# The last down-projection stage of the first FFN as seven products of sums of quarters, in a decoder trunk on one core

## The chip, the cores and the metric

The kernel runs on one core of one Trainium2 chip. The metric is device time in microseconds (us), the median of several executions. The core's engines work side by side, each through its own queue in order: TensorE (PE) multiplies matrices into PSUM, VectorE (DVE) and ScalarE (ACT) work on elements, GpSimd (POOL) and SyncE (SP) mostly issue transfers (DMA).

## What is computed

A decoder trunk of 512 tokens and width 1024: retention, gated ConvFFN, stick-breaking attention, gated ConvFFN, a final norm. All in float32. Only the FFN and its surroundings matter here:

```python
def _conv_ffn(h, w_up, conv_w, conv_b, w_down):
    u = h @ w_up
    u = lax.conv_general_dilated(u, conv_w[:, None, :].astype(u.dtype), window_strides=(1,),
                                 padding=[(CONV_W - 1, 0)],
    ...
    gate, val = jnp.split(u, 2, axis=-1)
    return (jax.nn.silu(gate) * val) @ w_down
    ...
        x = x + _conv_ffn(_rmsnorm(x, ffn_norm[i]), ffn_w_up[i], ffn_conv_w[i],
                          ffn_conv_b[i], ffn_w_down[i])
```

`D_FF` is 2816, so an FFN has 22 feature tiles of 128 (each a gate and a value of the up-projection), and the down-projection multiplies 22 x 128 features into 8 row tiles of x.

## The kernel before

**Precision.** Every float32 operand is split into `hi` (rounded to the matmul's type, a cast on ScalarE) and `lo` (the remainder, a subtraction on VectorE); a product is three matmuls, hi x hi, hi x lo, lo x hi.

**Layout.** x stands transposed: 8 tiles of 128 features x 512 tokens (`head` is tile 0, then x1 to x7; the rows below call all of them x). Weights come from HBM in chunks. `chunk` (L159 on) loads one into a `raw` slot on SyncE's queue, casts it to `hi` and subtracts for `lo`. Each of the three has a ring of five slots: four in a pool that lives as long as the kernel and a fifth, whose names carry a plus (`hi+`, `lo+`), in the pool of the present phase (`ret`, `ffn`, `sb`). When a phase ends, the next one's tiles take over its memory, and the fifth slot with them.

**An FFN** (`ffn`). `first4` multiplies the first two feature tiles' weights, eight k steps (one x tile each), into four banks. The other up-projections follow, 24 matmuls of 512 columns each. `ffn_act` evicts a bank, applies the three taps and the gate, and prepares the feature as an operand of the down-projection. The down-projection is done in three stages, features 0 to 7, 8 to 15 and 16 to 21 in the first FFN, and its result is added to x stage by stage. The first two are fast stages: `fast_down` computes, for each half of the rows of x (four tiles), seven products of sums of quarters in place of eight products of quarters, a Strassen scheme. A product has 256 token columns (`quarter`, L666), and the banks are added to or subtracted from x on VectorE (L676), 14 instructions of 256 columns per half. For that a pair of features needs 7 x 256 columns of operand: four quarters, and three further sums that VectorE forms (L645 to L647), then a cast (L649) and a subtraction (L650) of 1792 columns (`oh`, `ol`). The corresponding sums of weight quarters are formed ahead of time in HBM: `weight_sums` has POOL issue transfers, half of them accumulating, in the order of the table `ORDER`. The fast stages run two features after their last one.

The third stage is ordinary: a feature's operand is a cast and a subtraction of 512 columns (L637, L638), and `down` takes, for each of the 8 row tiles, one weight chunk of 128x768 and 18 matmuls of 512 columns, adds the bank to x (`add_to_x`, L228), and at once prepares the next norm from that tile: `norm_split` (L155 on ScalarE, L156 on VectorE: the tile times its gain, as hi and lo) and `norm_sum` (a square on ScalarE, L254, added up on VectorE, L255).

**What follows it.** `first4("sfirst")` of the stick-breaking layer takes one chunk and one split x tile in each k step. The norm's factor (one over a root of the mean square, one per token) is applied only to the results: `rsqrt` sums the squares over partitions with two matmuls on TensorE (L262), takes the root on ScalarE and the reciprocal on VectorE. It stands before the matmuls of one of the k steps.

**Order.** A scheduler arranges each engine's instructions when the program is built; on the chip each queue runs in the order so set.

Of the kernel before, what the change touches and what calls it, by code (L numbers as in the profile page):

```python
# [18 lines left out]
KD = D // P  # L19
# [6 lines left out]
NF = DFF // P  # L26
CH = 1024
STAGES = (((0, 8), (8, 16), (16, 22)), ((0, 8), (8, 14), (14, 18)))
FAST = (2, 2)
TAIL = 18  # L30
Q = S // 2
HALF = S // 2
# [1 line left out]

ORDER = (
    (("fqk", 0, 1), ("fv", 0, 2), ("fg", 0, 1), ("fqk", 1, 1), ("fg", 1, 1), ("fast0_0", 0, 2), ("fast0_1", 0, 2)),
    (("fast1_0", 0, 2), ("fast1_1", 0, 2)),
)
WARM = 3
RAW = 4  # L40
# [4 lines left out]
class Kernel:  # L45
# [133 lines left out]
    def first4(self, name, load=False):  # L179


        ps = [self.att() for _ in range(4)]
        for k in range(KD):
            w = self.wchunk(name, k, S)
            if load:
                if k:
                    self.nc.sync.dma_start(self.x[k], self.t["xT"][k])
                self.norm_split(k, 0, load)
                self.norm_sum(k)
            if k == (KD - 1 if load else KD // 2):  # L190
                self.r = self.rsqrt(self.sq, D, "rr")
            for i, (a, b) in enumerate(((0, 0), (1, 0), (0, 1))):
                for m in range(4):
                    self.nc.tensor.matmul(  # L194
                        ps[m], w[a][:, m * P : (m + 1) * P], self.xs[k][b], start=k + i == 0, stop=k == KD - 1 and i == 2
                    )
        return ps
# [426 lines left out]
    def ffn_act(self, l, f, ps):  # L624
# [7 lines left out]
        nc.vector.tensor_mul(y, g, v)  # L632
        if f >= STAGES[l][FAST[l] - 1][1]:
            if f % 2 == 0:
# [46 lines left out]
    def ffn(self, l, last):  # L681
        a, s = [], 0
        first = self.first4(f"ufirst{l}")
        if l == 0:
            self.weight_sums(ORDER[1], self.r)
        self.phase("ffn")
        for f in range(NF):
            a.append(self.ffn_act(l, f, first[2 * f : 2 * f + 2] if f < 2 else (None, None)))
            if f == 1:
                self.swap_pool()  # L690
            if s < 2 and f == STAGES[l][s][1] + 1:
                lo, hi = STAGES[l][s]
                for half in range(2):
                    self.fast_down(l, s, a[lo + 1 : hi : 2], half)
                s += 1
        self.swap_pool()
        self.down(l, a, s, last)
        if last is not None:
            self.phase("sb")
        return a  # L700
# [248 lines left out]
def _quarters(w, nk):  # L949

    n = w.shape[1] // (4 * P)
    w = w.reshape(nk, 2, P, n, 2, 2, P)
    return w.transpose(3, 5, 1, 2, 4, 0, 6).reshape(n, 4, P, 2 * nk * P)
# [15 lines left out]
def _layout(x, ret_norm, ret_w_in, ret_w_out, sb_norm, sb_w_in, sb_w_out,  # L969
# [26 lines left out]
    for l in range(2):  # L996
# [4 lines left out]
        for s, (lo, hi) in enumerate(STAGES[l]):  # L1001
            w = ffn_w_down[l][lo * P : hi * P]
            if s < FAST[l]:
                a[f"fast{l}_{s}"] = _quarters(w, (hi - lo) // 2)
# [29 lines left out]
```

## Time and profile before

| | before |
|---|---|
| median of 3 runs | 1352.93 us (1352.07 to 1353.94) |
| the profiled execution, time | 1353.2 us |
| the profiled execution, span | 1351.4 us |
| TensorE busy | 1337.1 us, 99% of the span |
| VectorE busy | 1012.0 us, 75% |
| ScalarE busy | 664.2 us, 49% |
| matmuls | 7086 |

Busy time of TensorE says that a matmul was under way; matmuls overlap (one of 512 columns shows 0.39 us), so their rate is read from the distance of their starts in the timeline. An engine's idle time counts only where TensorE waits for it in turn. Times in the rows are us from the span's start.

### The profile page before, as it was taken

The page shows a single profiled execution, that of the slowest core. Times are in us where ns is not written, and L with a number is a line of the kernel's source. Part 1 is how long each engine was busy: PE and PEld are TensorE (multiplying, and loading weights), DVE is VectorE, ACT ScalarE, POOL GpSimd, SP SyncE. Part 2 cuts the span into 40 slices and gives each one's busy share as a digit, 9 for nine tenths or more (in the row PEclk, how much of TensorE's full clock was granted, in tenths as well). Part 3 has the DMA queues.
Part 4 walks back from the last instruction along what each step waited for, and adds up shares of the span by engine and source line. Part 5 has one row for each costly group of instructions (what it writes and reads, how often), then busy time and mean ns, then how long its engine had stood idle before and what let it go on. Part 6 is the DMA issues. An engine that isn't in the chain of part 4 may idle for free.

```text
span 1351.4 us, 18540 instructions
## 1 busy us (share of the span) xinstructions
PE 1337.1 (99%) x7086; PEld 1142.2 (85%) x7086; DVE 1012.0 (75%) x1401; ACT 664.2 (49%) x987; POOL 111.4 (8%) x191
## 2 busy tenths in 40 slices
PE   9999999999999999999999999999999999999997
PEld 7888889899988889888988887777888899898887
DVE  7777677688769887678676628888699886787665
ACT  5444535574655444444344437666375443444434
POOL 1222221000002210000000011221000000000000
PEclk9999999999999999999999999999999999999999
DMA  9999999834338976334521654544143345235121
GB/s 319 302 292 279 278 305 293 257 106 154 102 123 269 284 203 188 109 94 123 166 72 47 186 142 146 148 117 111 40 141 109 97 140 157 84 111 173 53 70 63
DMA packets 67962, 217.96 MB, mean 161 GB/s; under 512 B 7969, under 2 KB 10145, under 8 KB 67873
## 3 DMA queue, kind: packets, MB, share of 16 engines
q1 hardware_dynamic: 45616, 145.97, 34.1%
q0 software_dynamic: 20736, 69.22, 20.7%
q10 hardware_dynamic: 1520, 1.58, 0.3%
q8 instruction: 56, 0.92, 0.3%
q14 instruction: 34, 0.27, 0.1%
HBM read 202.06 MB, written 58.72 MB: 193 GB/s over the span
## 4 chain that ended last, share of the span: by engine, by line
PE 96%; DVE 2%; ACT 1%; issue 0%; DMA 0%; DVEq 0%
PE acc L171 20%; PE acc L172 20%; PE acc L173 20%; PE att L194 7%; PE x L666 6%; PE att L666 5%; PE z L666 3%; PE acc L666 2%; PE att L374 2%; PE att L172 2%; PE att L171 2%; PE att L173 2%; PE one L789 1%; PE tp L781 1%; PE z L761 1%; DVE sg L766 1%
## 5 line engine op out<-in xcount | busy, mean ns | idle before, releaser
L164 ACT CAST hi<-raw 128x1024 fp32r<-128x1024 f32 (+2 forms) x255 | 248.1, 974 | 341.2 <-PE acc L172 184.2
L165 DVE TENSOR_TENSOR lo<-raw,hi 128x1024 fp32r<-128x1024 f32 (+2 forms) x255 | 285.4, 1123 | 74.6 <-ACT hi L164 73.0
L172 PE MATMUL acc<-xl,hi 128*128 128x512 f32 x696 | 271.3, 390 | 0.0
L171 PE MATMUL acc<-xh,hi 128*128 128x512 f32 x696 | 271.2, 390 | 0.0
L173 PE MATMUL acc<-xh,lo 128*128 128x512 f32 x696 | 271.1, 390 | 0.0
L173 PEld LDWEIGHTS acc<-xh,lo 128*128 128x128 f32 x696 | 130.7, 188 | 27.3
L171 PEld LDWEIGHTS acc<-xh,hi 128*128 128x128 f32 x696 | 130.7, 188 | 26.2
L172 PEld LDWEIGHTS acc<-xl,hi 128*128 128x128 f32 x696 | 130.7, 188 | 26.1 <-issue 0.2
L621 DVE SCALAR_TENSOR_TENSOR tt<-tt,vec,tt 128x511 f32<-128x511 f32 (+1 forms) x176 | 130.8, 748 | 3.9 <-ACT tt L619 1.4
L618 DVE TENSOR_TENSOR tt<-acc,rr 128x512 f32<-128x512 f32 x80 | 55.1, 689 | 73.0 <-PE acc L173 73.0
L619 ACT ACTIVATE tt<-tt,vec 128x512 f32<-128x512 f32 x88 | 71.5, 815 | 9.5 <-DVE tt L618 8.4
L666 PE MATMUL att<-xo,hi 128*128 128x256 f32 x384 | 70.1, 284 | 0.0
L228 DVE TENSOR_TENSOR x<-x,acc 128x512 f32<-128x512 f32 x63 | 42.9, 687 | 33.8 <-PE acc L173 33.8
L766 DVE TENSOR_TENSOR_SCAN sg<-sg,diag 128x512 f32<-128x512 f32 (+3 forms) x64 | 52.5, 821 | 13.2 <-ACT sg L763 13.2
L666 PEld LDWEIGHTS att<-xo,hi 128*128 128x128 f32 x384 | 59.8, 190 | 0.2
L628 ACT ACTIVATE tt<-tt 128x512 f32<-128x512 f32 x44 | 27.8, 631 | 55.2 <-DVE tt L621 55.2
L666 PE MATMUL att<-xo,lo 128*128 128x256 f32 x192 | 54.3, 283 | 0.0
L666 PE MATMUL x<-oh,hi 128*128 128x256 f32 x188 | 53.5, 285 | 0.0
L666 PE MATMUL x<-oh,lo 128*128 128x256 f32 x188 | 53.2, 283 | 0.0
L666 PE MATMUL x<-ol,hi 128*128 128x256 f32 x188 | 53.2, 283 | 0.0
L171 PE MATMUL acc<-hi,xh 128*128 128x512 f32 x120 | 46.7, 389 | 0.0
L172 PE MATMUL acc<-lo,xh 128*128 128x512 f32 x120 | 46.7, 389 | 0.0
(569 smaller groups left out, 2967.1 us busy)
## 6 DMA issues: line engine op xcount, KB each, us to landing
raw<-in_up SPq DMA_DIRECT2D x80, 512.0 KB, 4.2
raw<-sum SPq DMA_DIRECT2D x48, 512.0 KB, 4.3
sum<-in_fast POOLq DMA_DIRECT2D x36, 512.0 KB, 9.9
sum<-sum POOLq DMA_DIRECT2D x24, 512.0 KB, 8.0
raw<-in_fast SPq DMA_DIRECT2D x18, 512.0 KB, 3.6
raw<-in_rout SPq DMA_DIRECT2D x16, 512.0 KB, 5.9
sk<-hl POOLq DMA_DIRECT2D x32, 256.0 KB, 4.4
sum<-in_fqk POOLq DMA_DIRECT2D x12, 512.0 KB, 9.8
```

Of the source, the lines that this page charges most:

```text
L164: nc.scalar.copy(hi, raw)
L165: nc.vector.tensor_sub(lo, raw, hi.bitcast(F32))
L171: mm(out, a[0], b[0], start=start, stop=False)
L172: mm(out, a[0], b[1], start=False, stop=False)
L173: mm(out, a[1], b[0], start=False, stop=stop)
L194: self.nc.tensor.matmul(ps[m], w[a][:, m * P : (m + 1) * P], self.xs[k][b], start=k + i == 0, stop=k == KD - 1 and i == 2)
L228: self.nc.vector.tensor_add(self.x[m], self.x[m], ps)
L618: nc.vector.tensor_mul(u, ps, self.r)
L619: nc.scalar.activation(c, u, AF.Identity, scale=w[2], bias=w[3])
L621: nc.vector.scalar_tensor_tensor(c[:, i:], u[:, : S - i], w[2 - i], c[:, i:], op0=ALU.mult, op1=ALU.add)
L666: mm(out[:, :Q], a[ai], b[bi], start=start and k + i == 0, stop=k == nk - 1 and i == 2, skip_group_check=not start)
L766: nc.vector.tensor_tensor_scan(sg[:, :n][:, ::-1], sg[:, :n][:, ::-1], self.diag[:, S - n :][:, ::-1], 0.0, op0=ALU.mult, op1=ALU.max,)
```

## The change

The first FFN's third stage also becomes a fast stage. Its weights are laid out as quarters, and `weight_sums` forms their sums for it (`fast0_2`), ahead of those of the second FFN in the same call. `ffn_act` prepares features 16 to 21 in pairs (`FAST[0]` is now 3). After the last feature, `ffn` calls `fast_down` for both halves, and the norm's splits and squares of four tiles follow each half. In `first4("sfirst")` the factor `rsqrt` now stands before the last k step; before, it stood before step 4 of 0 to 7. The two up-projections' and the retention's keep their places.

```diff
-FAST = (2, 2)
+FAST = (3, 2)
...
-    (("fast1_0", 0, 2), ("fast1_1", 0, 2)),
+    (("fast0_2", 0, 2), ("fast1_0", 0, 2), ("fast1_1", 0, 2)),
...
-            if k == (KD - 1 if load else KD // 2):
+            if k == (KD // 2 if name == "ufirst0" or name == "ufirst1" else KD - 1):
                 self.r = self.rsqrt(self.sq, D, "rr")
...
-        self.swap_pool()
-        self.down(l, a, s, last)
+        if FAST[l] > s:
+            lo, hi = STAGES[l][s]
+            for half in range(2):
+                self.fast_down(l, s, a[lo + 1 : hi : 2], half)
+                for m in range(4 * half, 4 * half + 4):
+                    self.norm_split(m, last)
+                    self.norm_sum(m)
+            self.swap_pool()
+        else:
+            self.swap_pool()
+            self.down(l, a, s, last)
```

In weight chunks of 128x768 the stage takes 14 (7 per half) where it took 8. In the fast scheme the seven products write the banks x, z, x, acc (y in the code), x, z, x, two banks of 256 columns each time. The second half writes the same banks again.

Three places in the queues, before and after.

TensorE, start of the third stage, before. `oh_6503` and `ol_6504` hold features 20 and 21 as hi and lo; `acc_6595` is row tile 0, `acc_6627` row tile 1. The rows begin after the 12 matmuls on features 16 to 19:

```order
L171 MATMUL acc_6595<-oh_6503,hi_6590 128x512 [waits Activation_49]
L172 MATMUL acc_6595<-ol_6504,hi_6590 128x512 [waits DVE_49]
L173 MATMUL acc_6595<-oh_6503,lo_6591 128x512
L171 MATMUL acc_6627<-oh_5725,hi_6622 128x512 [waits DVE_49]
L172 MATMUL acc_6627<-ol_5726,hi_6622 128x512
L173 MATMUL acc_6627<-oh_5725,lo_6623 128x512
L171 MATMUL acc_6627<-oh_5725,hi_6622 128x512
L172 MATMUL acc_6627<-ol_5726,hi_6622 128x512
L171 MATMUL acc_6595<-oh_6503,hi_6590 128x512 [waits Activation_49]
```

and after the change. `oh_6608` and `ol_6609` are the pair of features 20 and 21 with its sums, `x_6612`, `x_6613`, `z_6614`, `z_6615`, `acc_6694` and `acc_6695` the banks of three products of the first half. The first row is the last of 36 matmuls on the two other pairs:

```order
L666 MATMUL acc_6695<-oh_6448,lo_6698 128x256
L666 MATMUL x_6612<-oh_6608,hi_6617 128x256 [waits Activation_49]
L666 MATMUL x_6613<-oh_6608,hi_6617 128x256
L666 MATMUL z_6614<-oh_6608,hi_6643 128x256
L666 MATMUL z_6615<-oh_6608,hi_6643 128x256
L666 MATMUL acc_6694<-oh_6608,hi_6697 128x256
L666 MATMUL acc_6695<-oh_6608,hi_6697 128x256
L666 MATMUL x_6612<-ol_6609,hi_6617 128x256 [waits DVE_49]
L666 MATMUL x_6612<-oh_6608,lo_6618 128x256
```

Before, the wait for feature 21 stands behind 20 matmuls of 512 columns, and other matmuls of row tile 1 stand beside it. After, the wait for the pair's hi part stands behind 36 matmuls of 256 columns, and that for its lo part six further on.

ScalarE, end of the third stage and start of `first4("sfirst")`, before. `hi_6861` is weight chunk 0 of `sfirst`; `xh` are the norm's splits, `tt` its squares:

```order
L155 ACTIVATE xh_6680<-x_90,vec 128x512 [waits DVE_49]
L254 ACTIVATE tt_6684<-x_90 128x512
L164 CAST hi_6861<-raw_6860 128x512 [waits DMAHW3_49,PE_49]
L155 ACTIVATE xh_6713<-x_91,vec 128x512 [waits DVE_49]
L254 ACTIVATE tt_6717<-x_91 128x512
L155 ACTIVATE xh_6746<-x_92,vec 128x512 [waits DVE_49]
L254 ACTIVATE tt_6750<-x_92 128x512
```

and after the change, where chunk 0 is `hi+_1290_7056` and `hi_7092`, `hi_7110` and `hi_7128` are chunks 2, 3 and 4:

```order
L164 CAST hi_7092<-raw_7091 128x512 [waits DMAHW2_49,DVE_49,PE_49]
L155 ACTIVATE xh_7015<-x_92,vec 128x512 [waits DVE_49]
L254 ACTIVATE tt_7019<-x_92 128x512
L164 CAST hi_7110<-raw_7109 128x512 [waits DMAHW3_49,PE_49,Activation_49]
L155 ACTIVATE xh_7022<-x_93,vec 128x512 [waits DVE_49]
L254 ACTIVATE tt_7026<-x_93 128x512
L155 ACTIVATE xh_7029<-x_94,vec 128x512
L254 ACTIVATE tt_7033<-x_94 128x512
L155 ACTIVATE xh_7036<-x_95,vec 128x512 [waits DVE_49]
L254 ACTIVATE tt_7040<-x_95 128x512
L164 CAST hi+_1290_7056<-raw_7055 128x512 [waits DMAHW7_49]
L164 CAST hi_7128<-raw_7127 128x512 [waits DMAHW4_49,PE_49,Activation_49]
```

Chunk 0's cast stood ahead of the splits of x3 to x7 (the names carry a buffer number: x_92 is x4, x_93 x5, x_94 x6, x_95 x7). Now it has the fifth slot of the ring and stands behind those of x4 to x7.

SyncE, the same place after the change; `raw_7055` is chunk 0, `raw_7145` chunk 5, the others chunks 1 to 4, 6 and 7 of `sfirst`, and the first row is the last chunk of the third stage:

```order
L163 DMA raw_6989<-in_fast_2 128x768 [waits DMAHW3_49,DVE_49]
L163 DMA raw_7073<-in_sfirst 128x512 [waits DMAHW5_49,DVE_49,Activation_49]
L163 DMA raw_7091<-in_sfirst 128x512 [waits DMAHW6_49,DVE_49]
L163 DMA raw_7109<-in_sfirst 128x512 [waits DMAHW7_49,DVE_49]
L163 DMA raw_7127<-in_sfirst 128x512 [waits DMAHW4_49,DMAHW0_49,DVE_49]
L163 DMA raw_7163<-in_sfirst 128x512 [waits DMAHW1_49,DVE_49]
L163 DMA raw_7181<-in_sfirst 128x512 [waits DMAHW2_49,DVE_49]
L163 DMA raw_7055<-in_sfirst 128x512
L163 DMA raw_7145<-in_sfirst 128x512 [waits DMAHW7_49,DVE_49]
```

Chunk 0's load is issued behind those of chunks 1 to 4, 6 and 7, each of which waits for VectorE to free a slot. Before, chunk 0 came first of the eight (it had an ordinary slot), and chunk 1 had the fifth slot.

## Rows read from the trace of the kernel before

**Rows 1.** The page: busy time, share and count of TensorE; its granted clock in 40 slices.

```profile
PE 1337.1 (99%) x7086; PEld 1142.2 (85%) x7086; DVE 1012.0 (75%) x1401; ACT 664.2 (49%) x987; POOL 111.4 (8%) x191
PEclk9999999999999999999999999999999999999999
```

**Rows 2.** Waits of TensorE, longest group: total us, times, longest us.

```profile
PE tp L781 <- DVE bt L770: 2.6, 4, 1.0
```

**Rows 3.** Timeline of TensorE, last down-projection stage: start us, us, engine line op.

```profile
711.03 0.39 PE L171 MATMUL acc<-xh,hi+_1192_6545 128*128 128x512 f32 x1
711.71 0.39 PE L171 MATMUL acc<-oh,hi 128*128 128x512 f32 x1
...
744.48 0.39 PE L173 MATMUL acc<-oh,lo 128*128 128x512 f32 x1
744.70 0.39 PE L194 MATMUL att<-xh,hi 128*128 128x512 f32 x1
```

**Rows 4.** Stretch of the second fast stage: its us, PE busy (matmuls), clock, DMA, GB/s.

```profile
627.80:668.00 40.20, 40.20 (x336) 1.00 0.59 170
```

**Rows 5.** Timeline of VectorE after the last up-projection.

```profile
711.91 0.69 DVE L618 TENSOR_TENSOR tt<-acc,rr 128x512 f32<-128x512 f32 x1 [2.32 <-PE acc L173]
712.55 0.96 DVE L165 TENSOR_TENSOR lo+_1228_6722<-raw,hi+_1227_6721 128x768 fp32r<-128x768 f32 x1
713.49 1.53 DVE L621 SCALAR_TENSOR_TENSOR tt<-tt,vec,tt 128x511 f32<-128x511 f32 x2
715.06 0.69 DVE L632 TENSOR_TENSOR ar<-tt,tt 128x512 f32<-128x512 f32 x1
```

**Rows 6.** By line, operand sums and conversion: count, ns min/median/max, first and last start.

```profile
L645 DVE TENSOR_TENSOR ar<-ar x15: 681/691/693, 426.6 to 1181.7; 128x512 f32<-128x512 f32 x15
...
L647 DVE SCALAR_TENSOR_TENSOR ar<-ar x15: 418/424/426, 429.3 to 1182.8; 128x256 f32<-128x256 f32 x15
...
L649 ACT CAST oh<-ar x15: 1680/1693/1705, 430.5 to 1183.7; 128x1792 fp32r<-128x1792 f32 x15
...
L650 DVE TENSOR_TENSOR ol<-ar,oh x15: 2024/2026/2029, 432.3 to 1185.5; 128x1792 fp32r<-128x1792 f32 x15
```

**Rows 7.** By line, an addition to x and a norm split's remainder.

```profile
L676 DVE TENSOR_TENSOR x<-x,x x56: 412/416/422, 504.2 to 1230.2; 128x256 f32<-128x256 f32 x56
...
L156 DVE SCALAR_TENSOR_TENSOR xl<-x,vec,xh x21: 744/751/754, 376.4 to 993.9; 128x512 fp32r<-128x512 f32 x21
```

**Rows 8.** Timeline of TensorE, first matmul of the second fast stage.

```profile
627.80 0.28 PE L666 MATMUL x<-oh,hi 128*128 128x256 f32 x1
```

**Rows 9.** Timeline of ScalarE, second FFN's norm: first and last of seven.

```profile
986.26 0.72 ACT L155 ACTIVATE xh<-x,vec 128x512 fp32r<-128x512 f32 x1
...
989.69 0.60 ACT L164 CAST hi+_1760_9196<-raw 128x512 fp32r<-128x512 f32 x1
```

**Rows 10.** DMA issues: queue, count, KB each, median us from issue to landing.

```profile
raw<-in_rqk SPq DMA_DIRECT2D x4, 512.0 KB, 12.0
...
sum<-in_fast POOLq DMA_DIRECT2D x12, 384.0 KB, 8.1
...
raw<-in_sfirst SPq DMA_DIRECT2D x8, 256.0 KB, 2.6
```

**Rows 11.** Timeline of POOL, its last sum transfer for layer 1.

```profile
493.50 0.82 POOL L411 DMA_DIRECT2D sum<-in_fast  x1 [2.61 <-DMA sum<-sum]
```

**Rows 12.** Timelines of VectorE and ScalarE, the norm's factor in stick-breaking.

```profile
759.13 3.35 DVE L266 RECIPROCAL rr<-tt 128x512 f32<-128x512 f32 x1 [0.85 <-ACT tt L264]
...
772.79 0.69 ACT L750 ACTIVATE sv<-acc,rc 128x512 f32<-128x512 f32 x1 [3.87 <-PE acc L173]
```

**Rows 13.** Timeline of TensorE, start of the kernel.

```profile
1.60 2.93 PE L300 MATMUL one<-diag,ones 128*128 128x256 f32 x6 [1.60 <-DVE diag L296]
7.38 1.91 PE L194 MATMUL att<-xh,lo 128*128 128x512 f32 x4
9.09 1.26 PE L194 MATMUL att<-xl,hi 128*128 128x512 f32 x4
```

## Prediction

> **What bounds the kernel now.** I read the page's busy times first: TensorE is busy 1337.1 us of a span of 1351.4, at full clock in every slice [rows 1]. So only two things can move the end: the time that TensorE's own instructions take, and waits of TensorE that are new. Next I read the list of waits: once the kernel has started, the longest single one is 1.0 us, and the largest group sums to 2.6 us [rows 2]; no load is in the list. Nothing is spare on TensorE that a new wait could be paid from, and nothing behind it makes up for one: a microsecond of waiting is a microsecond of the end.
>
> Then the timeline of the stage that changes. The last up-projection matmul issues at 711.48 (711.03 plus two steps); the down-projection runs from 711.71 to 744.70, where the next stage's first matmul issues: 32.99 us [rows 3]. It holds 8 row tiles of 6 features of 3 matmuls, 144 of 512 columns. One of them each (711.71 - 711.03) / 3 = 0.2267 us [rows 3], so 32.64 us is work and 0.35 us is lost.
>
> **What TensorE gains.** The new stage has 2 halves x 7 products x 2 row tiles x 3 pairs x 3 = 252 matmuls of 256 columns. In the second fast stage of the same layer 336 of these take 40.20 us without a pause [rows 4], 0.1196 each, more than half of 0.2267 (0.1134). 252 x 0.1196 = 30.15 us. The gain is 32.64 - 30.15 = 2.49, with the lost 0.35 it is 2.84 us, not the eighth (4.1 us) that seven for eight products suggest. The Trainium skill, "TensorE: Matmul & The Clock Gate", section "Back-to-back issue gap", gives N / 2.4 + 2.5 ns for a warm engine, 215.8 and 109.2 ns; an estimate by it is a gain of 3.56 for the matmuls, and the sum below would be 1.1 smaller. The rows' fixed part per matmul is larger, and with 108 more matmuls the rows decide.
>
> **The start: a new wait.** Before, a feature's conversion is one cast and one subtraction of 512 columns, and 20 matmuls of 0.2267 (15 on the other five features, 5 of the next tile) stand ahead of the first one that reads feature 21. Now the last pair (features 20 and 21) must first form its sums, and all three pairs enter every product. TensorE's order has 36 matmuls on the two ready pairs, then waits for ScalarE's `oh` (six matmuls), then for VectorE's `ol`. VectorE's chain after the last up-projection matmul, from the rows: evict at 711.91, the staging subtraction at 712.55, two taps at 713.49 to 715.02, product at 715.06 to 715.75 [rows 5]. This far it is the same in both kernels. Then 0.04 between dependent instructions (715.02 to 715.06 [rows 5]): difference 0.69 to 716.48, two of 0.42 to 717.40, ScalarE's cast of 1792 columns 1.69 to 719.13, VectorE's subtraction 2.03 to 721.19 [rows 6]. Six more instructions of 5.3 us stand where one cast and one subtraction of 512 columns stood. TensorE: 36 x 0.1196 = 4.31, done at 716.02; waits to 719.18, **3.16 us**; six matmuls to 719.90; waits to 721.24, **1.34 us**. Together 4.50. Bounds: 3.9 if TensorE's last step is released 0.3 sooner at each wait, 5.0 if another conversion slips in ahead on ScalarE.
>
> **The middle.** From 721.24 to the third product of the second half TensorE has 124 matmuls, 14.8 us. The sum of VectorE's work that must be done before that product may write its bank: 5 staging subtractions of 0.96 [rows 5], 15 additions of 0.42 and 4 norm splits of 0.75 [rows 7], 3 sums of squares of 0.69 (as the difference in [rows 6]): 16.2 us, less about 0.05 for each of 27 since the next one starts before the last ends (711.91 + 0.69 against 712.55 [rows 5]): 14.8. So VectorE is level with TensorE here, because the norm of the first four x tiles falls into the stage. I take 0.4 us of waits, bounds 0 and 1.3.
>
> **The end: a second new wait.** The next stage starts on weight chunk 0, and the six added chunks have turned the ring of five so that this chunk gets the fifth slot, which lies in memory of the phase that is just ending. The orders show what follows: ScalarE casts it behind all eight norm instructions of x4 to x7, and SyncE issues its load behind chunk 7's. x5 and x7 get their last addition only from the seventh product. Let E be when TensorE has issued its last product. The last matmul of that product's first row tile issues ten steps, 1.20 us, before; its result takes 0.28 [rows 8], and VectorE's addition of 0.42 [rows 7] makes x5 final at about E - 0.48. From there ScalarE runs split, square, split, square, split, square, cast: the same seven instructions take from 986.26 to 990.29, 4.03 us, where the next FFN begins [rows 9]. The cast is done at E + 3.58, TensorE starts at E + 3.65: **3.65 us** where before it went into the next stage at once. The `lo` half (0.69) is ready before the four `hi` matmuls (0.91) are done. The load is issued about E - 2.0 and lands 2.6 us later [rows 10]; ScalarE wants it at E + 3.0, a cover of 2.4 us. Bounds: 3.0 if the split of x4 is out of the way early, 4.3 if x5 is late by the waits of the middle.
>
> **What I cost at nothing.** The 16 added sum transfers stand ahead of layer 1's in POOL's queue, with nothing else behind them until layer 1 begins; POOL's last issue before is at 493.50 [rows 11], and 16 x 8.1 us [rows 10], one after the other behind it, would be 130 us, to 623, 88 us before the stage. Some now run beside the first fast stage, where a chunk lasts 24 x 0.1196 = 2.9 us; a load as slow as the retention's qk, 12.0 us [rows 10], is covered by the five chunks that stand converted ahead of it, 14 us. The norm's reciprocal square root, three k steps later: from VectorE's reciprocal at 759.13 to the first v eviction at 772.79 are 13.7 us, of which ScalarE's last 3.87 is waiting for TensorE [rows 12]; TensorE has the last k step and three v tiles, 2.7 + 3 x 5.4 = 19 us, before it needs that eviction. If this cover were gone, each late microsecond would count in full.
>
> **Sum.** -2.84 + 4.50 + 0.4 + 3.65 = +5.7 us. The profiled execution took 1353.2 us (span and 1.8 around it); the median is 1352.93, so 1358.6. The smallest terms give +4.1, the largest +7.8.
>
> **Rivals.**
> 1. *The end wait is hidden*, the case that is not slower. If chunk 0's cast ran before the norm's, as it did before (TensorE went from 744.48 to 744.70 with no gap [rows 3]), the sum would be +2.1, 1355.0, within 0.2%, which is 2.7 us and about what a measurement of this kernel can tell from no change. It decides when the end wait is under 0.6 us. Against it: the order of a queue is fixed, and x7's split stands ahead of that cast. 7%.
> 2. *The waits lower the clock.* TensorE's first matmuls, at 1.60, and those at 7.38 to 9.09 run at 0.4275 us for 512 columns, the lower of the two levels (1.2 and 2.4 GHz); by about 9.5 it has risen [rows 13]. After that no wait is over 1.0 us [rows 2] and the clock stays at full [rows 1], so no row shows what a wait of 3 us does. If the clock fell and took as long as at the start to rise, 7.9 us (9.5 - 1.60) at half speed would cost up to 3.9 us for each fall: 1362.5, or 1366 for two. The Trainium skill, the same page, section "What's actually happening", says: "the default state is throttled, and activity releases the throttle". By that rule this rival would come true if a wait counts as idle long enough. 14%.
> 3. *TensorE's arithmetic alone*: -2.84, 1350.1, if both conversions kept ahead. It needs both chains to be wrong. 2%.
> 4. *The added sums starve the first fast stage*: 512 KB per 2.9 us there, beside the sums. Against it speaks the retention, where loads of 12.0 us left no wait in TensorE's list. It decides when a load takes over the 14.4 us that five chunks cover; one half as slow again as the retention's, 18 us, would cost 3.6: 1362. 4%.
>
> **How the numbers follow.** The forecast has 73%, with its own range 1357.0 to 1360.7. The rivals take 27%. The range of 8 in 10 goes from 1356.2 to 1362.5, which leaves out rivals 1 and 3 and the double fall. Faster by over 0.2%: 0.02 (rival 3); within: 0.08 (rival 1 and a forecast at the smallest bounds); slower: 0.90.
>
> **What will show it.** In the changed profile: the L666 matmuls of the last stage at 0.12 us; TensorE waiting for `oh` for about 3 us and for `ol` for 1.3 soon after 716; the waits of the middle under 1.3 together; the first L194 matmul of the next stage waiting 3 to 4 us for the cast of `hi+`, with the norm's L155 and L254 ahead of it on ScalarE; the stage then ends near 750.4 instead of 744.7; all other stages shifted and unchanged. I am wrong if the order of waits on TensorE is another (a bank, a load), if matmuls after a wait space at 0.2 instead of 0.12, or if TensorE waits in the first fast stage.

## The result, and the profile after

The changed kernel takes 1363.41 us (median of 3 runs, 1361.35 to 1363.62) against 1352.93: the ratio is 1.0073, 95% interval 1.006 to 1.0086. It is slower, as predicted, but by 10.5 us where 5.7 was forecast, and 0.9 us above the range. (A ratio here is formed from all runs and need not be the quotient of the two medians; 1.0073 is 9.9 us.) The profiled execution has a span of 1361.8 us against 1351.4, so the trace holds the whole difference: 10.4 us.

The page of the changed kernel, TensorE's row and its granted clock in 40 slices, to be held against [rows 1]:

```profile
PE 1340.2 (98%) x7194; PEld 1149.9 (84%) x7194; DVE 1027.7 (75%) x1433; ACT 666.8 (49%) x990; POOL 122.5 (9%) x207
PEclk9999999999999999999998999999999999999999
```

There are 108 matmuls more, as counted, yet TensorE is busy 3.1 us longer where 2.5 us less work was forecast. The one slice with an 8 in the clock's row is the 22nd, 714.9 to 749.0 us: the changed stage. The list of TensorE's waits (total us, times, longest us), against [rows 2]:

```profile
PE att L194 <- ACT hi+_1290_7056 L164: 3.5, 1, 3.5
PE x L666 <- ACT oh L649: 3.0, 1, 3.0
PE tp L790 <- DVE bt L779: 2.6, 4, 1.0
...
PE x L666 <- DVE ol L650: 1.1, 1, 1.1
```

The three new waits are the three of the prediction, by name and nearly by size; the old group (`tp`) is what it was. The timeline of TensorE through the changed stage, against [rows 3] (start, duration, engine, line; in brackets the idle time and what ended it):

```profile
712.29 0.28 PE L666 MATMUL x<-oh,hi 128*128 128x256 f32 x1
712.41 0.28 PE L666 MATMUL x<-ol,hi 128*128 128x256 f32 x1
...
716.49 0.28 PE L666 MATMUL acc<-oh,lo 128*128 128x256 f32 x1
719.75 0.50 PE L666 MATMUL x<-oh,hi 128*128 128x256 f32 x2 [2.98 <-ACT oh L649]
...
721.81 0.58 PE L666 MATMUL x<-ol,hi 128*128 128x256 f32 x1 [1.08 <-DVE ol L650]
722.19 0.41 PE L666 MATMUL x<-oh,lo 128*128 128x256 f32 x1
722.40 0.41 PE L666 MATMUL x<-ol,hi 128*128 128x256 f32 x1
...
749.61 0.28 PE L666 MATMUL x<-oh,lo 128*128 128x256 f32 x1
753.37 1.19 PE L194 MATMUL att<-xh,hi+_1290_7056 128*128 128x512 f32 x4 [3.48 <-ACT hi+_1290_7056 L164]
754.79 2.07 PE L194 MATMUL att<-xh,lo+_1291_7057 128*128 128x512 f32 x4 [0.23 <-DVE lo+_1291_7057 L165]
...
758.31 1.09 PE L194 MATMUL att<-xh,hi 128*128 128x512 f32 x4
```

The stage now lasts from 712.29 to 753.37, 41.08 us where it lasted 32.99. By the starts, the waits are 3.14, 1.24 and 3.64 us (each gap less one step of 0.12; the last matmul ahead of the second wait starts at 720.44). The work is 252 x 0.1196 = 30.14. That leaves 41.08 - 30.14 - 8.02 = 2.92 us, and the rows from 722.19 show most of it: a matmul of 256 columns starts 0.21 us after the one before, where 712.41 - 712.29 is 0.12. Up to 727.52 these steps make 2.6 us. In the next stage the first twelve matmuls of 512 columns run from 753.37 to 758.31, 4.94 us instead of 12 x 0.2267 = 2.72: another 2.2. Of this 1.8 lies in longer steps, and 0.4 by the starts (0.2 by the profile) is a wait for the chunk's low half. The sum is -2.85 + 8.02 + 2.92 + 2.22 = 10.3, the whole difference.

The windows of the changed kernel around the first wait and around the last one (length, busy time and count of each engine, the granted clock after the parenthesis of POOL, DMA share, GB/s):

```profile
719.00:719.75 0.75, 0.00 (x1) 0.00 (x1) 0.02 (x1) 0.69 (x1) 0.00 (x0) 1.00 0.00 0
719.75:721.00 1.25, 0.97 (x6) 0.77 (x6) 1.25 (x1) 0.00 (x0) 0.00 (x0) 0.87 0.00 0
722.00:724.00 2.00, 2.00 (x10) 2.00 (x11) 1.35 (x4) 1.13 (x2) 0.00 (x0) 0.50 0.00 0
726.00:727.00 1.00, 1.00 (x7) 1.00 (x6) 1.00 (x2) 0.00 (x0) 0.00 (x0) 0.50 0.66 92
728.00:729.00 1.00, 1.00 (x11) 1.00 (x10) 0.81 (x3) 1.00 (x2) 0.00 (x0) 1.00 0.83 197
...
752.00:753.30 1.30, 0.00 (x0) 0.00 (x0) 1.30 (x3) 1.30 (x4) 0.00 (x0) 1.00 0.00 0
753.30:754.00 0.70, 0.63 (x3) 0.55 (x4) 0.70 (x2) 0.54 (x2) 0.00 (x0) 1.00 0.00 0
755.00:756.00 1.00, 1.00 (x3) 0.81 (x4) 1.00 (x3) 0.00 (x0) 0.00 (x0) 0.50 0.19 61
758.00:759.00 1.00, 1.00 (x5) 0.84 (x4) 0.00 (x0) 0.49 (x1) 0.00 (x0) 0.88 1.01 385
```

While TensorE waits, the granted clock is still 1.00. It falls to 0.50, the lower of the two levels (1.2 GHz of 2.4), soon after TensorE has resumed, and comes back some microseconds later. In both stretches TensorE is slow, and idle only for the waits of 1.08 and 0.23 us that are listed anyway, so no list of waits names this loss.

ScalarE's timeline ahead of the last wait shows the queue that was predicted, the norm's split (L155) and square (L254) of each tile ahead of chunk 0's cast:

```profile
749.30 0.72 ACT L155 ACTIVATE xh<-x,vec 128x512 fp32r<-128x512 f32 x1 [0.31 <-DVE x L676]
749.93 0.61 ACT L254 ACTIVATE tt<-x 128x512 f32<-128x512 f32 x1
...
752.72 0.60 ACT L164 CAST hi+_1290_7056<-raw 128x512 fp32r<-128x512 f32 x1
```

VectorE formed the chunk's low half only behind the norm's last sum, which it began at 753.45. That is the wait for the low half above:

```profile
754.05 0.68 DVE L165 TENSOR_TENSOR lo+_1291_7057<-raw,hi+_1290_7056 128x512 fp32r<-128x512 f32 x1
```

### The profile page after: what moved, and what is told of

Its sections match the earlier page's. It is cut to its first block, busy times and chain, and to the rows that moved or that the text cites. A ratio compares the mean times of both kernels' runs of the same rounds, so it can differ in the third digit from the quotient of the medians.

```text
span 1361.8 us, 18853 instructions
## 1 busy us (share of the span) xinstructions
PE 1340.2 (98%) x7194; PEld 1149.9 (84%) x7194; DVE 1027.7 (75%) x1433; ACT 666.8 (49%) x990; POOL 122.5 (9%) x207
## 4 chain that ended last, share of the span: by engine, by line
PE 95%; DVE 3%; ACT 1%; issue 0%; DMA 0%; DVEq 0%
PE acc L172 19%; PE acc L171 19%; PE acc L173 19%; PE x L666 8%; PE att L194 7%; PE att L666 5%; PE z L666 4%; PE acc L666 3%; PE att L374 2%; PE att L172 2%; PE att L171 1%; PE att L173 1%; PE one L798 1%; PE tp L790 1%; PE z L770 1%; DVE sg L775 1%
## 5 line engine op out<-in xcount | busy, mean ns | idle before, releaser
L164 ACT CAST hi<-raw 128x1024 fp32r<-128x1024 f32 (+2 forms) x260 | 252.1, 972 | 356.2 <-PE acc L172 183.3
L165 DVE TENSOR_TENSOR lo<-raw,hi 128x1024 fp32r<-128x1024 f32 (+2 forms) x260 | 291.0, 1122 | 79.2 <-ACT hi L164 76.9
L172 PE MATMUL acc<-xl,hi 128*128 128x512 f32 x706 | 275.3, 390 | 0.0
L171 PE MATMUL acc<-xh,hi 128*128 128x512 f32 x706 | 275.2, 390 | 0.0
L666 PE MATMUL x<-oh,hi 128*128 128x256 f32 x222 | 63.8, 288 | 3.1 <-ACT oh L649 3.0
L666 PE MATMUL x<-ol,hi 128*128 128x256 f32 x222 | 64.0, 288 | 1.1 <-DVE ol L650 1.1
L666 PE MATMUL x<-oh,lo 128*128 128x256 f32 x222 | 63.8, 287 | 0.0
L228 DVE TENSOR_TENSOR x<-x,acc 128x512 f32<-128x512 f32 x56 | 38.0, 685 | 25.4 <-PE acc L173 25.4
L666 PEld LDWEIGHTS x<-oh,hi 128*128 128x128 f32 x222 | 43.3, 195 | 3.8 <-ACT oh L649 3.2
L666 PEld LDWEIGHTS x<-ol,hi 128*128 128x128 f32 x222 | 43.6, 197 | 1.5 <-DVE ol L650 1.3
```

What stands on the lines that cost most here:

```text
L164: nc.scalar.copy(hi, raw)
L165: nc.vector.tensor_sub(lo, raw, hi.bitcast(F32))
L171: mm(out, a[0], b[0], start=start, stop=False)
L172: mm(out, a[0], b[1], start=False, stop=False)
L228: self.nc.vector.tensor_add(self.x[m], self.x[m], ps)
L666: mm(out[:, :Q], a[ai], b[bi], start=start and k + i == 0, stop=k == nk - 1 and i == 2, skip_group_check=not start)
```

## The experiments

Theory A: each wait of about 3 us costs its own length, and then the microseconds that TensorE works at the lower clock. Theory B: the waits cost their length, and the 5.1 us left over (2.92 and 2.22) have another cause in these stages, such as the memory traffic of VectorE, ScalarE and the loads.

**1. The moved square root alone.** The kernel before, with only this edit:

```diff
-            if k == (KD - 1 if load else KD // 2):
+            if k == (KD // 2 if name == "ufirst0" or name == "ufirst1" else KD - 1):
```

> The kernel before with one edit of the change alone: the norm's reciprocal square root ahead of the stick-breaking stage is formed behind the last k step instead of the fifth. The prediction priced this at nothing, with a cover of 19 us: 1352.9, within 0.2% of before (ratio 0.999 to 1.001). The rival: the first v eviction comes late and every late microsecond counts, so about 1 to 3 us slower, with a new wait of TensorE on VectorE or ScalarE behind the first matmuls of v.

Measured: 1353.16 us against 1353.17, ratio 0.9999 (0.999 to 1.0008). The list of TensorE's waits has the same group at its head, 2.6 us. This part of the change is free, as priced.

**2. The ring of staging slots turned by one.**

```diff
+        for tag in self.tiles:
+            self.tiles[tag] = (self.tiles[tag] + 1) % 5
         first = self.first4("sfirst")
```

> The changed kernel with the ring of staging slots turned one slot further before the next stage, so that weight chunk 0 gets an ordinary slot and is cast ahead of the norm. Theory A (the waits lower the granted clock, and TensorE then works at the lower level for some microseconds): the end wait of 3.6 us goes and with it the slow matmuls behind it, 1.9 us, so 1363.4 - 5.5 = 1357.9, and the granted clock stays at 1.00 from 745 to 760. Theory B (the waits cost their own length, and the rest of the loss is something else in the stage): 1363.4 - 3.6 = 1359.8, and the first matmuls of the next stage still space at 0.43 us.

Measured: 1357.1 us against 1353.17, ratio 1.0029 (1.0017 to 1.0042). From 1.0073 that is 0.0044, 6.0 us less, where theory A says 5.5 (3.64 + 2.22 by the starts above would be 5.9) and theory B 3.6. By the two intervals the 6.0 lies between about 3.5 and 8.4, so the time alone does not decide; the windows do. TensorE's waits on `oh` and `ol` remain, that on `hi+` is gone; the windows at the start of the next stage:

```profile
PE x L666 <- ACT oh L649: 3.0, 1, 3.0
```

```profile
748.00:752.00 4.00, 4.00 (x25) 3.38 (x24) 3.94 (x8) 3.69 (x8) 0.20 (x4) 1.00 0.63 194
752.00:756.00 4.00, 4.00 (x19) 3.33 (x18) 4.00 (x7) 3.13 (x6) 0.00 (x0) 1.00 0.10 22
```

With the wait, the slow matmuls behind it went too: VectorE is as busy in these windows (3.94 and 4.00 of 4) as in the changed kernel (3.95 and 4.00), and TensorE keeps its full clock. Behind the first wait, which stayed, the clock fell as before: 0.50 from 720 to 724.

**3. The first wait filled with work that nobody needs.**

```diff
                 self.fast_down(l, s, a[lo + 1 : hi : 2], half)
+                if half == 0:
+                    self.fill(34, a[lo + 1][0])
...
+    def fill(self, n, x):
+        ps = self.one()
+        for _ in range(n):
+            self.nc.tensor.matmul(ps[:, :Q], self.ones, x[:, :Q], start=True, stop=True)
```

> The changed kernel with 34 matmuls of 256 columns more on TensorE whose result nobody reads: by the order, 24 of them stand ahead of the first matmul that waits for the last pair's cast and 10 ahead of the first that waits for its low half, 2.9 and 1.2 us of work, about as long as the two waits. They save no wait; they only keep TensorE busy. Theory A: the clock does not fall, the stage's matmuls stay at 0.12 us throughout, and the 3.0 us that were lost between 720 and 728 come back: 1360.4. Theory B (the matmuls of that stretch are slow for another reason, such as memory traffic of VectorE, ScalarE and the loads beside them): no gain, 1363.4 or a little more, and spacings of 0.21 us stay from 720 to 728.

Measured: 1359.61 us against 1353.17, ratio 1.0051 (1.0037 to 1.0066): 0.0022 or 3.0 us less than the changed kernel, as theory A has it. By the two intervals that is about 0.3 to 5.6, so here too the trace says more than the time. Its waits, its first matmuls on the last pair, and its windows at the start of the stage and behind the end wait:

```profile
PE att L194 <- ACT hi+_1291_7091 L164: 3.5, 1, 3.5
...
PE x L666 <- ACT oh L649: 0.2, 1, 0.2
```

```profile
718.45 0.50 PE L666 MATMUL x<-oh,hi 128*128 128x256 f32 x2 [0.17 <-ACT oh L649]
```

```profile
716.00:720.00 4.00, 3.83 (x33) 3.62 (x32) 2.21 (x3) 1.69 (x1) 0.00 (x0) 1.00 0.00 0
720.00:724.00 4.00, 4.00 (x34) 3.89 (x33) 3.41 (x8) 1.72 (x3) 0.00 (x0) 1.00 0.01 4
724.00:728.00 4.00, 4.00 (x36) 4.00 (x35) 3.98 (x9) 2.26 (x3) 0.00 (x0) 1.00 0.66 201
...
749.00:750.00 1.00, 0.38 (x1) 0.38 (x2) 1.00 (x3) 1.00 (x3) 0.00 (x0) 0.68 0.00 0
```

The needed matmuls start no earlier than in the changed kernel: the first on the last pair comes 7.46 us after the stage's first (718.45 - 710.98) in both (719.75 - 712.29). The 34 added ones only stand where TensorE idled. From the first start to the last the stage takes 34.87 us instead of 37.31, so 2.44 of the 2.92 came back and 0.5 did not. VectorE does as much beside them as before, and still the clock stays at 1.00 and 33 to 36 matmuls of 256 columns fit in 4 us. Theory B falls here: what made them slow was the idleness ahead of them. The end wait was left in, and behind it the clock fell as before.

**4. An added wait in the kernel before.** Nothing of the change is in this one. At two places a weight chunk is cast behind a chain of small VectorE operations; the lines that make it:

```diff
+    def late(self, n):
+        t = [self.sb("tt") for _ in range(2)]
+        self.nc.vector.tensor_scalar(t[0], self.x[KD - 1], 0.0, None, op0=ALU.mult)
+        for i in range(n):
+            self.nc.vector.tensor_scalar(t[(i + 1) % 2], t[i % 2], 0.0, None, op0=ALU.mult)
+        return t[n % 2][:, :1]
...
+            nc.scalar.activation(hi, raw, AF.Identity, bias=late)
```

> The kernel before, nothing of the change in it, with an added wait of TensorE at two places: the second weight chunk of the stick-breaking stage and of the second FFN's first up-projection is cast behind a chain of 10 and 6 small VectorE operations that starts from the last tile of x (the values do not change). By an estimate from a 512-column operation of VectorE (0.4 to 0.7 us) less the 2.7 us of matmuls on the first chunk, the waits are 2 to 5 us and 0.5 to 2.5 us. Theory A: the time grows by the sum of both waits and by 2 to 3 us more for each that is about 3 us long, with the granted clock under 0.8 in the 4 to 8 us behind it and 512-column matmuls at 0.43 there; a wait of 1 us or less leaves the clock at 1.00. Theory B: the time grows by the waits alone, and matmuls behind them space at 0.227.

Measured: 1381.89 us against 1353.17, ratio 1.0211 (1.0197 to 1.0225). As a measure of one wait it missed: the norm's square root, and in the second FFN its whole chain, fell in behind the added operations, so there were seven new waits, the longest of them these:

```profile
PE one L273 <- ACT tt L153: 9.6, 2, 8.3
PE att L205 <- ACT hi+_1265_6891 L175: 6.6, 1, 6.6
```

```profile
752.00:756.00 4.00, 0.00 (x0) 0.00 (x0) 3.90 (x3) 0.72 (x2) 0.00 (x0) 0.50 0.02 7
756.00:760.00 4.00, 2.73 (x7) 2.15 (x7) 2.54 (x8) 0.72 (x1) 0.00 (x0) 0.50 0.21 65
```

It shows that the lower clock comes without the new stage: 512-column matmuls start every 0.43 us behind both places. As the price of one wait it says nothing.

**5. One clean wait, of three lengths.** The chain is put where VectorE is mostly idle, behind the third v tile of the stick-breaking stage in the kernel before, and holds up the fifth tile's first chunk. `late` here takes the tile from which its chain starts. Three kernels differ in the length of the chain (15, then 12 and 13):

```diff
-            w = [self.wchunk("sv", 4 * c + a) for a in range(4)]
+            w = [self.wchunk("sv", 4 * c + a, CH, self.late(out[2]) if c and a == 0 else None) for a in range(4)]
```

> The kernel before, nothing of the change in it, with a chain of 15 operations of VectorE (512 columns, 0.45 us each, as the run of the first added wait showed) behind the third v tile of the stick-breaking stage; the fifth v tile's first weight chunk is cast behind it (the values do not change). The wait that this gives TensorE, worked out from the rows: 0.9 for the tile's result and eviction, 15 x 0.453, 1.1 for the cast, less 5.44 us of matmuls on the fourth tile and 0.9 of four matmuls that the order brings forward: 2.5 us. Theory A: if a wait of 2.5 us is long enough, the granted clock is at 0.5 in a stretch behind it, with 512-column matmuls at 0.43 us for 4 to 8 us, and the time grows by the 2.5 and by 1 to 3 more; if not, by 2.5 alone. Theory B: by 2.5 alone, matmuls at 0.227 throughout.

> The same added wait in the kernel before, with a chain of 12 operations of VectorE instead of 15. With 15 TensorE waited 3.5 us (1 more than estimated) and the granted clock was lower behind it; 3 x 0.453 less is a wait of 2.1 us. The waits of 1.2 to 1.4 us in the other runs left the clock at 1.00, those of 3.0 to 3.6 did not, so this one decides a gap between them. If it leaves the clock alone, matmuls behind it start every 0.227 us and the time grows by about 2.1, less the 0.9 of work brought forward: 1354 to 1355. If it lowers it, spacings of 0.43 follow for some microseconds and the time is 1 to 2 more.

> The same with a chain of 13: a wait of about 2.6 us. The same two cases: 1354.5 to 1355.5 with the clock at 1.00, or 1 to 2 more with a stretch of 0.43 us spacings behind the wait.

Measured: with 15, 1357.57 us against 1353.61, ratio 1.0026 (1.0012 to 1.004); with 12, 1354.19 against 1352.97, 1.0013 (1.0004 to 1.0023); with 13, 1357.0, 1.0035 (1.0022 to 1.0048). Each kernel's wait and windows, first 12, then 13, then 15:

```profile
PE acc L180 <- ACT hi L173: 1.9, 1, 1.9
```

```profile
788.00:792.00 4.00, 1.83 (x7) 0.97 (x6) 2.76 (x4) 4.00 (x6) 2.03 (x4) 1.00 0.34 68
792.00:796.00 4.00, 4.00 (x19) 3.30 (x18) 3.89 (x4) 3.97 (x6) 0.00 (x0) 1.00 1.00 248
```

```profile
PE acc L180 <- ACT hi L173: 3.7, 1, 3.7
```

```profile
793.00:794.00 1.00, 0.42 (x2) 0.38 (x3) 1.00 (x2) 1.00 (x2) 0.10 (x1) 1.00 0.85 188
795.00:796.00 1.00, 1.00 (x3) 0.81 (x4) 1.00 (x2) 1.00 (x2) 0.00 (x0) 0.50 1.07 287
```

```profile
PE acc L180 <- ACT hi L173: 3.5, 1, 3.5
```

```profile
793.00:794.00 1.00, 0.00 (x0) 0.00 (x0) 0.45 (x2) 1.00 (x2) 1.00 (x3) 1.00 0.88 176
796.00:797.00 1.00, 1.00 (x3) 0.83 (x3) 1.00 (x2) 1.00 (x2) 0.00 (x0) 0.50 1.16 315
```

The wait of 1.9 us (2.04 by the starts) left the clock at 1.00 and no slow matmul behind it. Its cost by the medians, 1.2 us (1.8 by the ratio, 0.5 to 3.1), agrees with the wait and a shorter one for the low half, 0.47, less 1.2 that the wait group on `tp` became smaller (1.4 instead of 2.6). The four matmuls brought forward may be the reason for that; it was not tried. The waits of 3.5 and 3.7 us lowered the clock for 3.4 us each, and the longer steps there make 1.8 and 1.5 us. For 12, 13 and 15 operations waits of 2.1, 2.6 and 2.5 us had been expected. The step from 12 to 13 was not the 0.45 us intended: ScalarE's table load (1.28 us) and a sigmoid (0.60) slipped in ahead of the late cast. So nothing here lies between 2.0 and 3.0 us. These kernels have neither the new stage nor its traffic, and the one with 12 differs from the others only in the chain: the waits alone do it.

**6. The waits taken out.** Three kernels with the ring turned as in 2. The first has other cuts between the stages (the last stage gets four pairs):

```diff
-STAGES = (((0, 8), (8, 16), (16, 22)), ((0, 8), (8, 14), (14, 18)))
+STAGES = (((0, 8), (8, 14), (14, 22)), ((0, 8), (8, 14), (14, 18)))
```

> The changed kernel with the ring turned by one slot, and with the first FFN's stages cut at features 8 and 14 instead of 8 and 16: its last stage has four pairs, 54 matmuls instead of 36 stand ahead of the wait for the last pair, and the number of matmuls is the same. The wait for the cast shrinks by 18 x 0.1196 = 2.15 us to about 0.9, that for the low half stays at about 1.1. Theory A (waits of about 3 us lower the clock, those of 1 us do not): no fall, so before's 1352.9 - 2.8 for the matmuls + 2.0 = 1352.1, within 0.2% of before. Theory A with a fall after two waits of 1 us: 1354 to 1355. Theory B (the stage has slow matmuls for another reason): the same 3 us slower, 1355.

The second converts the last pair in two pieces:

```diff
+        own = l == 0 and f == NF - 1
+        if own:
+            convert(4, 3)
...
-        nc.scalar.copy(hi, part(0, 7))
-        nc.vector.tensor_sub(lo, part(0, 7), hi.bitcast(F32))
+        convert(0, 4 if own else 7)
```

> The changed kernel with the ring turned, and the last pair converted in two pieces: the three quarters that need no difference first (768 columns), the four with differences (1024 columns) after. By the order TensorE then waits four times for shorter pieces where it waited twice. The first wait: the cast of 768 columns by about 716.6 against 716.0, 0.5 us; the low half and the second piece 0.5 to 1.5 us more together. Theory A: no wait near 3 us, so the clock stays up, and 1352.9 - 2.8 + 1.0 to 2.0 = 1351.1 to 1352.1. Theory B: 3 us more, 1354 to 1355.

The third has both edits:

> Both edits of the two other kernels together, with the ring turned: four pairs in the last stage, and the last pair converted in two pieces. TensorE reaches the last pair's first piece after 43 matmuls, at about 716.9, when its cast is done; the second piece is wanted at 719.4 and done at about 719.5. Waits of 0.2 to 1 us in all. The gain of the matmuls is then left nearly whole: 1352.9 - 2.8 + 0.5 = 1350.6, ratio about 0.998, by theory A. By theory B 1353.5.

Measured, against 1353.61 us of before: four pairs 1353.64, ratio 1.0 (0.9987 to 1.0013); two pieces 1353.84, 0.9997 (0.9985 to 1.0009); both 1350.97, **0.9977 (0.9966 to 0.9988)**, the one version that is faster than the kernel before. TensorE's waits on the last pair, with four pairs (and the windows around them) and then with two pieces; the third kernel has none of them in its list, and its longest group is the old one:

```profile
PE x L666 <- ACT oh L649: 1.2, 1, 1.2
PE x L666 <- DVE ol L650: 1.1, 1, 1.1
```

```profile
708.00:710.00 2.00, 0.79 (x7) 0.58 (x5) 0.26 (x1) 1.69 (x1) 0.00 (x0) 1.00 0.01 2
710.00:712.00 2.00, 0.97 (x6) 0.77 (x6) 1.99 (x1) 0.00 (x0) 0.00 (x0) 1.00 0.00 0
```

```profile
PE x L674 <- ACT oh L649: 0.5, 1, 0.5
PE x L674 <- DVE ol L650: 0.5, 1, 0.5
```

```profile
PE tp L798 <- DVE bt L787: 2.8, 5, 1.0
```

With four pairs the two waits are 1.40 and 1.24 us by the starts, 2.06 us apart, and the granted clock is 1.00 in each window around them. -2.85 + 2.64 is -0.2: a ratio of 0.9998, inside the measured interval. Theory B's 1355 would be 1.0016, outside it. With two pieces TensorE waits four times, 0.53 to 0.65 us each by the starts, 2.3 in all: twice on the last pair, once on a chunk's low half (the middle has less slack without the first wait), once on x in the next stage. That makes -0.5, ratio 0.9996. It agrees with what was measured, but the gain is smaller than the 0.8 to 1.8 us expected. The time alone does not refute theory B here (1354 to 1355, 1.0008 to 1.0016, against an upper end of 1.0009); the clock at 1.00 in the windows of the stage does. With both edits the gap on the last pair is 0.23 us, and -2.85 + 0.23 = -2.6 is a ratio of 0.998: nearly the whole gain of the matmuls.

## Why the prediction was wrong in size and right in sign

- **TensorE's gain, -2.84.** Right: at full clock, 256-column matmuls start every 0.12 us in the changed stage, and the version with hardly any wait got the gain. The Trainium skill ("TensorE: Matmul & The Clock Gate", "Back-to-back issue gap") would have had 0.109 by its formula, which it calls that of an isolated matmul; the measured step decides here too.
- **The start, 4.50.** Right: 3.14 + 1.24 = 4.38 against 3.16 + 1.34. The chain counted as six instructions has five; the 5.3 us are theirs.
- **The middle, 0.4.** 0: with the first wait filled, the rest of the stage has no gap on TensorE. VectorE, level with TensorE by the sum, kept up.
- **The end, 3.65.** Right: 3.64, for the predicted reason, and gone with another slot. That the low half would be ready in time was wrong: it stood behind the norm's last sum on VectorE and cost another 0.4 us.
- **At nothing.** Right for the square root (ratio 0.9999). The added sum transfers are in all versions that came out by the sum, and no wait of the first fast stage is in the list: rival 4 is false.
- **The sum, and the range. This is the step that failed.** The sum had no term for the clock after a wait. That stood apart as rival 2, with 14%, because "no row shows what a wait of 3 us does", and the range left out the double fall. It came true at both places: 2.92 us behind the first wait and its follower, of which filling the wait gave back 2.4, and 2.22 behind the last, of which 1.8 lies in slow steps and 0.4 in the wait for the low half. The rows show the sign that the prediction had named for being wrong, matmuls at 0.2 instead of 0.12 us behind a wait. The rival's place and mechanism were right; its price, up to 3.9 each from the start of the kernel [rows 13], was a bound and proved too large, which is why 1366 was too high and a single fall's 1362.5 too low. The sum with measured sizes: -2.85 + 4.38 + 0 + 3.64 + 2.92 + 2.22 = +10.3; 1352.93 + 10.3 = 1363.2 against 1363.41.
- **How it should have been weighed.** Three waits of over 1 us were forecast in a kernel whose longest had been 1.0 [rows 2]; that the clock had stayed up through those said nothing of waits three times as long, and the only rows with an idle TensorE behind them [rows 13] had the lower level, by their steps of 0.4275 us. (The 9 of the first slice [rows 1] says nothing against it: the trace holds no entry of the clock before 9.5 us, and the view shows 1.00 where it has none.) The sentence of the Trainium skill, "TensorE: Matmul & The Clock Gate", "What's actually happening", that the prediction quotes ties the lower level to the lack of activity; the trace agrees for waits of 3.0 us and more (0.50 behind each), and shows 1.00 behind those of 2.0 us and less. So 14% was too little for this rival.

## What to carry to other kernels

Price a new wait of the engine that bounds the kernel twice: by its length, and by what the clock takes back when work resumes; here the clock took some 2.4 us behind the waits of the first stage, 1.8 behind the last one and 1.5 to 1.8 behind a single added wait of 3.5 or 3.7, while the clock stayed up behind waits of 2.0 us and less. A new conversion ahead of a stage wants either more ready work in front of it or to be cut so that its first piece is early; here the two together, with the ring turned, made -0.2% of +0.7%, and each alone with the ring turned came out level with the kernel before. When stages get more chunks, look at which slot of the ring the next stage's first chunk falls on.

## What the runs showed of the hardware

The clock did not fall when a wait of 3.0 to 3.7 us began, but near its end: 1.00 up to 719.75 and 0.50 by 721.00 in the changed kernel, 1.00 until 754.00 and 0.50 by 755.00 at its end. By the windows the fall came 0.1 to 1.5 us after TensorE had resumed in five of the six such waits of these runs. In the kernel with the filled start it came 0.3 us before: the window from 749.00 to 750.00 has 0.38 us of work and a mean clock of 0.68. In the run with waits of over 6 us it fell while TensorE stood still: 2 us into the wait of 8.3 us, and within half a microsecond of the start of the one of 6.6, which followed two short waits.

How long it stayed low differed, too. It was about 7 us in the changed stage, with the ring turned as without (to about 727.5 and 726.8), where a second wait fell into the slow stretch. It was 3 to 4 us behind the four others (from about 755 to 758 in the changed kernel). Whether the second wait prolonged it, or the 256-column matmuls of that stage did, was not tried.
